# A projection as seven half-size products per pair of units, with its operand sums made by a paired LayerNorm

## The chip, the cores and the metric

The kernel runs on one core of a Trainium2 chip. The metric is device time in microseconds (us) of one execution. The names of the engines are those of the profile: PE is TensorE (matrix products), PEld its weight loads, DVE is VectorE, ACT is ScalarE, POOL is GpSimd and SP is SyncE, which here only issues DMAs. L192 is line 192 of the kernel before.

## The reference, cut to what matters

One inference step of a decoder layer for two request groups with shared weights: a prompt of 1024 tokens and eight samples of eight tokens each, all in fp32. The model width is 1024.

```python
def layernorm(x, g, b):
    mu = mean(x, axis=-1); var = mean(square(x - mu), axis=-1)
    return (x - mu) * rsqrt(var + EPS) * g + b

xn = rmsnorm(x, norm1_g)
q, k, v, glu_a, glu_b, gate_a, gate_b = split(xn @ w_in)
attn = sliding_window_attention(q, k, v)
branch_a = attn @ w_o_attn                            # 1024 x 1024, "o" below
u = glu_a * sigmoid(glu_b)
c = depthwise_conv_31(u)
branch_b = silu(layernorm(c, ln_b_g, ln_b_b)) @ w_pb  # 1024 x 1024, "pb" below
merged = sigmoid(gate_a) * branch_a + sigmoid(gate_b) * branch_b
h = x + merged @ w_out                                # 1024 x 1024, "out" below
y = h + ConvFFN(rmsnorm(h, norm2_g))
```

This is a sketch of the code; a final RMSNorm and the new caches are outputs too.

## The kernel before, in words

All 1024 + 64 tokens are handled together as T = 1088 columns; the 1024 channels lie on 8 tiles of 128 partitions (KT = 8). A matrix product in fp32 is made of three products of fp32r operands: every operand is split into a high part h, made by a cast on ACT, and a low part l, made by a subtraction on DVE (`split_ps`, L224 to L226), and `mm3` (L188 to L192) issues h by h, h by l and l by h. A unit is one tile of 128 output channels with its 128 x 1024 weights. `stream` (L194) runs a unit over the token chunks of 384, 384 and 320 columns (`CHUNKS`), 8 input tiles each, so 72 matmuls; an `evac` function takes each PSUM bank when it is complete. `weight` and `w_split` (L171, L172) load and split the weights of coming units. PSUM has four banks for each of the two tags "mm" and "aux". With the table `QUARTERS` the chunks are four of 272 columns (QW); HALF is 544.

The work is laid out as a list of units for PE. Side work is put on an agenda: `tick` is called once per three matmuls, and `plan` gives steps the tick at which they are emitted. Emission order is the order of priority; `later(n)` gives work a later place by n. Each engine and each DMA queue works strictly in its order.

The stages around the change follow each other on PE:

1. The last gate units of the input projection. Gates and intermediate results go to DRAM (d_ga, d_gb).
2. `phase_y`: eight units "o" (`do_o`, L977). Each multiplies its PSUM chunks with sigmoid(gate_a) and stores the product ma to d_ma on POOL's queue. Beside it runs LayerNorm, as side work in eight blocks of 136 tokens (`ln_steps`): load 8 channel tiles of the conv result from DRAM (d_c, L566), sum over the tiles by three additions (`reduce`, L554), a matmul with a constant matrix for the mean over the 128 partitions (L561), subtraction of the mean (L572), squares on ACT, sums and the second mean matmul, reciprocal root, multiplication (L587), eight Silu activations (L589) and the split into the tiles sh and sl. A block's three steps are 6 and 8 ticks apart, blocks are 15 ticks apart, and the first block begins 4 ticks before the first unit "o".
3. `phase_z`, units "pb" (`do_pb`): each loads its whole row of gate_b (L1011) and of ma (L1014) on SP's queue, 544 KB each, and each chunk's evac multiplies with the sigmoid (L1018), adds ma (L1019) and splits the sum into the quarter tiles mh and ml.
4. Units "out" over quarters: x is loaded per chunk (xr2), added to the PSUM result as H (L1061), and squares are summed for the second RMSNorm. The last four units go chunk by chunk, each chunk followed by `norm2`.
5. The FFN. Its up projection has three plain pairs of units and then 19 Strassen-Winograd pairs: two units are taken as a 2 x 2 matrix of blocks, and seven half-size products on sums of blocks stand for eight. The down projection is done so in part; there the residual H comes back from d_h by accumulating DMAs on POOL's queue (L1434).

## Time and profile before

| | us |
|---|---|
| median of 3 runs | 1664.97 |
| lowest, highest | 1664.64, 1666.62 |
| span of the profiled execution | 1662.4 |
| stage "o" with LayerNorm (637.12 to 735.91) | 98.79 |
| stage pb (735.91 to 830.79) | 94.88 |
| stretch of Strassen-Winograd pairs (1000.00 to 1105.40) | 105.40 |
| PE busy over the span | 1652.5 |

The profile is of one execution, whose own time is the span, from its first to its last instruction; it is 2.6 us shorter than the median, which is a device time of other executions. A stage is bounded by the start of its first matmul and that of the next stage's first. A group row gives the line, engine, operation, output and input, shapes and count, then busy time, mean nanoseconds of one instruction, and the idle time of its engine before them with what ended it. DMA rows give the kilobytes of one transfer and the median time from issue to landing.

### The profile page before, as it was taken

How to read it: one execution, taken by the hardware profiler on the slowest of the kernel's cores; microseconds unless marked ns; L12 is line 12 of the kernel's file. 1: busy time of each engine (PE TensorE's matmuls, PEld its weight loads, DVE VectorE, ACT ScalarE, POOL GpSimd, SP SyncE). 2: the span in 40 equal slices, each digit the busy share in tenths (PEclk: the TensorE clock that was granted, in tenths of full speed). 3: DMA queues.
4: the chain of work that ended last, by engine and by line, in shares of the span. 5: the costliest groups of instructions: out<-in, count | busy, mean ns of one | idle time of the engine just before them, and what ended most of it. 6: DMA issues, size and time to landing. Idle time of an engine off the chain costs nothing.

```text
span 1662.4 us, 29877 instructions
## 1 busy us (share of the span) xinstructions
PE 1652.5 (99%) x11550; PEld 1636.9 (98%) x11550; DVE 1337.3 (80%) x2432; ACT 866.3 (52%) x1781; POOL 290.2 (17%) x483
## 2 busy tenths in 40 slices
PE   9999999999999999999999999999999999999998
PEld 9999999999999999999999999999999999999997
DVE  7899979999989986855545896777887786988867
ACT  6424368774488845973233454444444454524222
POOL 0100112231011111110000171344444320000000
PEclk9999999999999999999999999999999999999999
DMA  6221212232121265544343332244444324766403
GB/s 208 84 71 42 75 60 81 99 103 86 55 53 48 77 227 168 178 154 145 106 155 108 80 125 103 97 113 115 112 114 111 94 103 134 243 168 168 118 14 108
DMA packets 98623, 187.09 MB, mean 113 GB/s; under 512 B 22848, under 2 KB 57680, under 8 KB 98464
## 3 DMA queue, kind: packets, MB, share of 16 engines
q1 hardware_dynamic: 79152, 125.18, 24.3%
q0 software_dynamic: 18896, 59.72, 11.9%
q8 instruction: 91, 1.49, 0.4%
q14 instruction: 52, 0.43, 0.1%
q10 hardware_dynamic: 432, 0.27, 0.1%
HBM read 129.75 MB, written 57.35 MB: 113 GB/s over the span
## 4 chain that ended last, share of the span: by engine, by line
PE 91%; DVE 5%; ACT 2%; DMA 1%; issue 1%; ACTq 0%; DVEq 0%; SPq 0%
PE mm L190 23%; PE mm L192 23%; PE mm L191 23%; PE aux L190 6%; PE aux L192 6%; PE aux L191 6%; PE aux L406 1%; DVE c L520 1%; PE aux L418 1%; PE aux L419 1%; PE aux L396 1%; PE aux L397 1%; DVE bt L520 1%; DVE q L739 1%; DMA bw<-d_b 0%
## 5 line engine op out<-in xcount | busy, mean ns | idle before, releaser
L190 PE MATMUL mm<-xh,whi 128*128 128x384 f32 (+1 forms) x904 | 301.1, 333 | 0.0
L191 PE MATMUL mm<-xl,whi 128*128 128x384 f32 (+1 forms) x904 | 295.4, 327 | 0.1
L192 PE MATMUL mm<-xh,wlo 128*128 128x384 f32 (+1 forms) x904 | 295.4, 327 | 0.0
L191 PEld LDWEIGHTS mm<-xl,whi 128*128 128x128 f32 x904 | 170.0, 188 | 1.6 <-DVE xl L277 0.7
L190 PEld LDWEIGHTS mm<-xh,whi 128*128 128x128 f32 x904 | 169.8, 188 | 0.7
L192 PEld LDWEIGHTS mm<-xh,wlo 128*128 128x128 f32 x904 | 169.7, 188 | 0.1
L190 PE MATMUL mm<-mh,whi 128*128 128x272 f32 (+4 forms) x428 | 125.9, 294 | 0.0
L191 PE MATMUL mm<-ml,whi 128*128 128x272 f32 (+4 forms) x428 | 125.1, 292 | 0.0
L192 PE MATMUL mm<-mh,wlo 128*128 128x272 f32 (+4 forms) x420 | 123.5, 294 | 0.0
L1172 DVE SCALAR_TENSOR_TENSOR acc<-st,fc,acc 128x1104 f32<-128x1104 f32 x88 | 119.8, 1364 | 2.8 <-ACT acc L1170 2.0
L171 ACT CAST whi<-wraw 128x1024 fp32r<-128x1024 f32 (+1 forms) x76 | 74.2, 981 | 79.8 <-PE mm L191 59.7
L520 DVE SCALAR_TENSOR_TENSOR bt<-u,consts,bt 128x513 f32<-128x513 f32 x120 | 89.8, 748 | 0.7
L520 DVE SCALAR_TENSOR_TENSOR c<-sm,hsum,c 128x512 f32<-128x512 f32 x120 | 89.6, 747 | 0.7
L172 DVE TENSOR_TENSOR wlo<-wraw,whi 128x1024 fp32r<-128x1024 f32 (+1 forms) x76 | 86.1, 1136 | 4.9 <-ACT whi L171 4.6
L520 DVE SCALAR_TENSOR_TENSOR c<-u,consts,c 128x512 f32<-128x512 f32 x112 | 83.7, 747 | 0.5
L190 PEld LDWEIGHTS mm<-mh,whi 128*128 128x128 f32 x428 | 80.5, 188 | 0.2
L191 PEld LDWEIGHTS mm<-ml,whi 128*128 128x128 f32 x428 | 80.6, 188 | 0.0
L192 PEld LDWEIGHTS mm<-mh,wlo 128*128 128x128 f32 x420 | 79.0, 188 | 0.0
L1152 POOL COPY st<-co 128x16 f32<-128x16 f32 x44 | 75.6, 1724 | 0.2 <-issue 0.2
L191 PE MATMUL mm<-tl,whi 128*128 128x272 f32 x240 | 69.6, 290 | 0.0
L1320 ACT COPY st<-mm 128x272 f32<-128x272 f32 (+2 forms) x133 | 44.6, 349 | 47.8 <-PE mm L192 47.8
L192 PE MATMUL mm<-th,whi 128*128 128x272 f32 x240 | 69.3, 289 | 0.0
(462 smaller groups left out, 5491.6 us busy)
## 6 DMA issues: line engine op xcount, KB each, us to landing
wraw<-wall SPq DMA_DIRECT2D x118, 512.0 KB, 3.8
bw<-d_b SPq DMA_DIRECT2D x42, 272.0 KB, 3.4
d_b<-gd POOLq DMA_DIRECT2D x36, 272.0 KB, 6.1
d_b<-acc POOLq DMA_DIRECT2D x24, 272.0 KB, 3.3
ar<-wdn SPq DMA_DIRECT2D x32, 192.0 KB, 4.3
d_g<-acc POOLq DMA_DIRECT2D x10, 544.0 KB, 4.3
ga<-d_ga SPq DMA_DIRECT2D x8, 544.0 KB, 4.0
gb<-d_gb SPq DMA_DIRECT2D x8, 544.0 KB, 3.6
```

The source lines that it names most:

```text
L171: self.cast = self.nc.scalar.copy(h[:, z], r[:, z]).ins
L172: self.nc.vector.tensor_tensor(l[:, z], r[:, z], h[:, z].bitcast(F32), ALU.subtract)
L190: mm(ps, wh, xh, start=first, stop=False, skip_group_check=more)
L191: mm(ps, wh, xl, start=False, stop=False, skip_group_check=more)
L192: mm(ps, wl, xh, start=False, stop=last, skip_group_check=more)
L396: nc.tensor.matmul(ps[:, j, :], q[g][:, h, qs], kd[g][:, keys], start=True, stop=False)
L397: nc.tensor.matmul(ps[:, j, :], q[g][:, h, qs], kl[g][:, keys], start=False, stop=True)
L406: nc.tensor.transpose(ps[:, h * P:(h + 1) * P], pt[:, h, kb * P:(kb + 1) * P], self.ident)
L520: mac = lambda o, x, w: nc.vector.scalar_tensor_tensor(o, x, w, o, ALU.mult, ALU.add)
L1152: nc.gpsimd.tensor_copy(ss[:, :, 0:2], co[:, f, 2:].rearrange("p (b t) -> p b t", b=NB))
L1172: nc.vector.scalar_tensor_tensor(acc, st[:, k:k + AW], fw(f, k), acc, ALU.mult, ALU.add)
L1320: op(d, r(ps))
```

## The change

pb becomes Strassen-Winograd's scheme, as in the FFN's up projection. Units 2p and 2p+1 form the output rows, the two halves of the input channels (4 tiles each) the inner blocks and the two halves of the tokens (544 columns) the output columns. Each of four pairs makes seven products; a product is a 128 x 512 block of weights by 512 channels x 544 tokens, done as two quarters of 272 columns, 24 matmuls. The weight operands are A11, A12, A22 and four sums made on DVE (`plan_pair`), each split into one slot of a ring of four, three products ahead. The other operands are the quadrants 11, 21 and 22 of the LayerNorm result and four sums T1 to T4.

LayerNorm makes those: `ln_steps` handles blocks i and i + 4 together, the two token halves at the same place, in 272 columns, and `ln_apply` writes three split quadrants and makes the sums with four subtractions of 544. T1 and T2 stay in SBUF (tiles w0 to w3), T3 and T4 go to DRAM (d_t) on POOL's queue and are loaded back on SP's. All four are split beside pair 0 (`t_split`). The pairs are planned from the start of the last gate unit, 30 ticks apart.

In pb (`pair`) three products are copied to an accumulator row in SBUF by ACT, the others are added on DVE, multiplied with the gate there, and the ma row in DRAM is added by an accumulating DMA on POOL's queue; the split of the result is emitted three products later. The gates come as 32 loads of 272 columns in a ring of five (`gate_load`) with a sigmoid each. In the output projection the first unit takes its quarters in the order 2, 3, 0, 1, x is loaded in whole rows, and H is stored as it is completed.

```diff
+GATE_AFTER = 30
+SPLIT_AFTER = 3
...
-LN_STEPS = (0, 6, 14)
-LN_LEAD = -4
-LN_SPACING = 15
+LN_STEPS = (0, 16, 26)
+LN_SPACING = 30
...
+            ct = live["ct"] = self.t(self.lt, [P, KT, 2 * n], "ct", bufs=2)
+            for x, r in zip(both, each(ct)):
+                nc.sync.dma_start(r, self.d_c[:, :, x * n:x * n + n].rearrange("k p t -> p k t"))
+            for y, r in enumerate(each(ct)):
+                reduce(y, r, self.t(self.cv, [P, 4, n], "u", bufs=2))
...
-            nc.vector.tensor_tensor(ct, ct, ps[:, None, :n].to_broadcast([P, KT, n]), ALU.subtract)
-            sq = self.t(self.cv, [P, KT, n], "c")
-            nc.scalar.activation(sq, ct, AF.Square)
-            reduce(sq, sq)
+            nc.vector.tensor_tensor(ct, ct, ps[:, None, :].to_broadcast([P, KT, 2 * n]), ALU.subtract)
+            for y, r in enumerate(each(ct)):
+                sq = self.t(self.cv, [P, KT, n], "c")
+                nc.scalar.activation(sq, r, AF.Square)
+                reduce(y, sq, sq)
...
+        j, d = i // 2, slice(i % 2 * n, i % 2 * n + n)
+        (r11, r21), (r12, r22) = [[ct[:, 4 * z:4 * z + 4, y * n:y * n + n] for z in range(2)] for y in range(2)]
+        for b, r in (("11", r11), ("21", r21), ("22", r22)):
+            h, l = self.sb[b][j]
+            self.split_ps(h[:, :, d], l[:, :, d], r)
+        w = self.t(self.xw, [P, 2, KT // 2, n], f"w{i}")
+        self.ln_words.append(w)
+        sub = lambda o, x, y: nc.vector.tensor_tensor(o, x, y, ALU.subtract)
+        sub(w[:, 0], r12, r11)
+        sub(r12, r22, r12)
+        sub(w[:, 1], r22, w[:, 0])
+        sub(r21, r21, w[:, 1])
+        nc.gpsimd.dma_start(self.d_t[0, j][:, :, d], r12)
+        nc.gpsimd.dma_start(self.d_t[1, j][:, :, d], r21)
...
+            if n == self.n_in - 1:
+                steps = []
+                for x in range(KT // 2):
+                    steps += self.ln_steps(x, self.now + x * LN_SPACING)
+                self.plan(steps)
...
+              for b in ("11", "22", "21")}
+        self.ln_words = []
+        self.w_stop = self.order.index(("pb", 0))
...
-        steps = []
-        for x in range(KT):
-            steps += self.ln_steps(x, self.now + LN_LEAD + x * LN_SPACING, sh, sl)
-        self.plan(steps)
...
-        def do_pb(m):
-            t = self.t(zt, [P, T], "gb", bufs=2)
-            nc.sync.dma_start(t, self.d_gb[m])
-            nc.scalar.activation(t, t, AF.Sigmoid)
-            r = self.t(zt, [P, T], "mar", bufs=2)
-            nc.sync.dma_start(r, self.d_ma[m])
-
-            def ev(c, o, n, ps):
-                cs = slice(o, o + n)
-                nc.vector.tensor_tensor(t[:, cs], ps[:, :n], t[:, cs], ALU.mult)
-                nc.vector.tensor_tensor(r[:, cs], r[:, cs], t[:, cs], ALU.add)
-                for z, (qo, qn) in enumerate(QUARTERS):
-                    lo, hi = max(o, qo), min(o + n, qo + qn)
-                    if lo < hi:
-                        d = slice(lo - qo, hi - qo)
-                        self.split_ps(mh[z][m // 4][:, m % 4, d], ml[z][m // 4][:, m % 4, d], r[:, lo:hi])
-
-            self.stream(("pb", m), xs, ev)
-
-        for m in range(KT):
-            do_pb(m)
...
+        stage = {}
+        for x in range(2, 4):
+            for j in range(2):
+                stage[x, j] = self.t(mp, [P, KT // 2, QW], f"mh{2 * x + j - 4}1")
+                nc.sync.dma_start(stage[x, j], self.d_t[x - 2, j])
...
+        def t_split(x):
+            for j in range(2):
+                if x >= T3:
+                    tt[x, j] = [self.t(*((xw, [P, KT // 2, QW], f"w{2 * j + y}") if x == T4 else
+                                         (tb, [P, KT // 2, QW], f"t{x}{j}{y}")), F32R) for y in range(2)]
+                h, l = tt[x, j]
+                for z in range(2):
+                    if x < T3:
+                        d, r = (slice(None), slice(None), slice(z * n, z * n + n)), self.ln_words[2 * j + z][:, x]
+                    else:
+                        d = (slice(None), slice(2 * z, 2 * z + 2))
+                        r = stage[x, j][d]
+                    self.split_ps(h[d], l[d], r)
+                    casts.append(self.cast)
+                    lows.append(self.low)
...
+            def split(name, *ops):
+                def go():
+                    if name == "a11":
+                        raws()
+                    for d, x, y, op in ops:
+                        nc.vector.tensor_tensor(live[d], live[x], live[y], op)
+                    i = len(ring)
+                    w = self.t(self.wp, [P, DM], ("whi", "wlo")[i % 2] + str((one + i // 2) % 2), F32R, bufs=1)
+                    with ExitStack() as es:
+                        if i == 2:
+                            es.enter_context(tc.issue_after(casts[3]))
+                            es.enter_context(tc.issue_after(lows[3]))
+                        self.split_ps(w[:, :hw], w[:, hw:], live[name])
+                    ring.append((w[:, :hw], w[:, hw:]))
+                return go
+
+            preps.extend([
+                split("a11"),
+                split("a21", ("a11", "a11", "a21", ALU.subtract), ("a21", "a21", "a22", ALU.add)),
+                split("a21", ("a21", "a22", "a11", ALU.subtract)),
+                split("a21", ("a21", "a12", "a21", ALU.subtract)),
+                split("a11"), split("a12"), split("a22")])
...
+        def gate_load():
+            if len(loaded) < len(gates):
+                m, c = gates[len(loaded)]
+                t = self.t(zt, [P, QW], "gb", bufs=5)
+                nc.sync.dma_start(t, self.d_gb[m][:, c * QW:c * QW + QW])
+                loaded.append(t)
+
+        def gate_open():
+            for _ in range(2):
+                x = len(ready)
+                t = ready[gates[x]] = loaded[x]
+                with tc.issue_after(casts[7]):
+                    nc.scalar.activation(t, t, AF.Sigmoid)
...
+        def pair(p, hooks):
+            acc = [self.t(mp, [P, T], f"ml{2 * (p % 2) + u}1") for u in range(2)]
+            banks = {}
+
+            def place(u, half, j):
+                return acc[u][:, (2 * half + j) * QW:(2 * half + j + 1) * QW]
+
+            def copy(u, half, ps):
+                with tc.issue_after(casts[3]):
+                    for j in range(2):
+                        nc.scalar.copy(place(u, half, j), ps[j])
+
+            def gate(u, half, ps, plain):
+                m, cs = 2 * p + u, slice(half * HALF, half * HALF + HALF)
+                gs = [ready[m, 2 * half + j] for j in range(2)]
+                xs = [place(u, half, j) for j in range(2)]
+                for x, y, g in zip(xs, ps, gs):
+                    if plain:
+                        nc.vector.tensor_tensor(x, y, g, ALU.mult)
+                    else:
+                        nc.vector.tensor_tensor(x, x, y, ALU.add)
+
+                def rest():
+                    if not plain:
+                        for x, g in zip(xs, gs):
+                            nc.vector.tensor_tensor(x, x, g, ALU.mult)
+                    nc.gpsimd.dma_start(acc[u][:, cs], self.d_ma[m][:, cs], accum_op=ALU.add)
+                    gate_load()
+                    gate_load()
+
+                def parts():
+                    for j in range(2):
+                        self.split_ps(*row(m, 2 * half + j), place(u, half, j))
+
+                with self.later(GATE_AFTER):
+                    rest()
+                due.append((7 * p + k + SPLIT_AFTER, parts))
+
+            seq = [
+                ("A", "11", True, 0, 0, copy), ("E", T1, True, 1, 1, copy), ("A", T2, False, 0, 1, copy),
+                ("E", "22", False, 0, 1, gate), ("A", T3, False, 1, 1, gate), ("C", "21", True, 0, 0, gate),
+                ("A", T4, False, 1, 0, gate)]
+            for k, (bank, b, fresh, u, half, op) in enumerate(seq):
+                prep(7 * p + k + 1 + AHEAD)
+                wh, wl = ring[7 * p + k]
+                for j in range(2):
+                    if fresh:
+                        banks[bank, j] = self.bank("mm" if bank == "A" else "aux")
+                    ps = banks[bank, j]
+                    xh, xl = B[b](j)
+                    for x in range(KT // 2):
+                        ks = slice(x * P, (x + 1) * P)
+                        self.mm3(ps[:, :QW], wh[:, ks], wl[:, ks], xh[:, x, :], xl[:, x, :],
+                                 fresh and x == 0, x == KT // 2 - 1, not fresh)
+                op(u, half, [banks[bank, j][:, :QW] for j in range(2)], *((b == T4,) if op is gate else ()))
+                if 2 <= k < 6:
+                    gate_open()
+                for go in hooks.get(k, ()):
+                    go()
+                while due and due[0][0] <= 7 * p + k:
+                    due.pop(0)[1]()
+
...
+        def out_ahead():
+            self.w_hl += [None] * (n_out - len(self.w_hl))
+            self.w_used, self.w_stop, self.slot = n_out, len(self.order), slot
+            self.w_load()
+            self.w_load()
+            self.w_split()
+            for m in range(2):
+                x_load(m)
...
+        for p in range(4):
+            plan_pair(p)
+        for _ in range(5):
+            gate_load()
+        prep(2)
+        t_split(T1)
+        hooks = [{0: [lambda: t_split(T2)], 2: [lambda: t_split(T3)], 4: [lambda: t_split(T4)]}, {},
+                 {2: [lambda: last_rows(2)]}, {2: [lambda: last_rows(3)], 4: [out_ahead]}]
+        for p in range(4):
+            pair(p, hooks[p])
+        while due:
+            due.pop(0)[1]()
...
+        for m in range(KT - OUT_TAIL):
+            for x in (m + 1, *(tail[2 * m - 4:2 * m - 2] if m > 1 else ())):
+                x_load(x)
+            self.stream(("out", m), xm, ev_out(m), chunks=(range(4), (2, 3, 0, 1))[m == 0], table=QUARTERS)
+            nc.gpsimd.dma_start(self.d_h[m], H[m])
```

161 lines of the change are left out of this document (94 added, 67 removed).

## The prediction

> **What bounds the kernel now.** I read the page's busy times first, then the waits of TensorE, then a table of busy times by stage, then the start times of single matmuls at the borders of the changed stage.
>
> ```profile
> span 1662.4 us, 29877 instructions
> ## 1 busy us (share of the span) xinstructions
> PE 1652.5 (99%) x11550; PEld 1636.9 (98%) x11550; DVE 1337.3 (80%) x2432; ACT 866.3 (52%) x1781; POOL 290.2 (17%) x483
> ```
>
> ```profile
> PE mm L629 <- DVE warm L622: 1.1, 1, 1.1
> PE mm L190 <- DVE H L1456: 0.9, 1, 0.9
> PE aux L418 <- ACT pth L225: 0.8, 1, 0.8
> ```
>
> ```profile
> 637.12:735.91 98.79, 98.79 (x610) 98.54 (x609) 75.27 (x108) 88.26 (x127) 12.98 (x24) 1.00 0.47 146
> 735.91:830.79 94.88, 94.88 (x578) 94.88 (x577) 48.28 (x101) 32.36 (x64) 0.54 (x1) 1.00 0.42 140
> ...
> 1000.00:1105.40 105.40, 105.40 (x839) 105.40 (x838) 80.51 (x125) 50.33 (x99) 31.86 (x60) 1.00 0.35 111
> ```
>
> The three wait rows are all the listed waits of TensorE, 2.8 us in the whole span, and none lies near the changed work. So time is matmul issue time, and any wait of TensorE that the change creates is paid in full. The last three rows give, by stage, the length and then the busy time with instructions of PE, PEld, DVE, ACT, POOL: the attention projection with LayerNorm beside it, the projection pb, and a stretch of Strassen-Winograd pairs of the FFN. In all three PE is busy throughout, with the clock at 1.00.
>
> ```profile
> 735.91 0.33 PE L190 MATMUL mm<-sh,whi 128*128 128x384 f32 x1
> 736.09 0.34 PE L191 MATMUL mm<-sl,whi 128*128 128x384 f32 x1
> ...
> 830.64 0.31 PE L192 MATMUL mm<-sh,wlo 128*128 128x320 f32 x1
> 830.79 0.29 PE L190 MATMUL mm<-mh,whi 128*128 128x272 f32 x1
> 830.92 0.29 PE L191 MATMUL mm<-ml,whi 128*128 128x272 f32 x1
> ```
>
> pb runs from 735.91 to 830.79: 576 matmuls (8 units, 3 chunks, 8 input tiles, 3 partial products) in 94.88 us, 0.165 us each. Matmuls overlap: one of 384 columns lasts 0.33 us but the next starts 0.18 us later. Durations must not be multiplied by counts here; stretches must.
>
> **The change, part by part.**
>
> *Matmuls of pb.* Four pairs of seven products of 24 matmuls, 672 of 272 columns, replace 576 of 384 and 320. The FFN row has 839 matmuls, nearly all of 272 columns, in 105.40 us: 0.1256 us each. 672 x 0.1256 = 84.4 us. Saved: 94.88 - 84.4 = 10.5 us. One product takes 3.01 us, a pair 21.1 us. The saving holds as long as TensorE is fed.
>
> *LayerNorm's mean matmuls.* Sixteen of 136 columns become eight of 272: the same columns, taken at nothing; they are TensorE's own work either way, some 0.2 us each now, so at most 1 us either way.
>
> *VectorE and ScalarE in pb.*
>
> ```profile
> L1018 DVE TENSOR_TENSOR gb<-mm,gb 128x384 f32<-128x384 f32 x16 | 8.9, 557 | 23.3 <-PE mm L192 21.2 <-ACT gb L1012 2.1
> L226 DVE TENSOR_TENSOR ml<-mar,mh 128x272 fp32r<-128x272 f32 x15 | 6.6, 439 | 8.3 <-ACT mh L225 8.3
> L225 ACT CAST mh<-mar 128x272 fp32r<-128x272 f32 x15 | 6.1, 410 | 3.8 <-DVE mar L1019 3.8
> L226 DVE TENSOR_TENSOR whi<-s,whi 128x512 fp32r<-128x512 f32 x10 | 6.9, 688 | 12.0 <-ACT whi L225 11.8
> L1264 DVE TENSOR_TENSOR s<-wraw 128x512 f32<-128x512 f32 x6 | 4.1, 691 | 1.9 <-DMA wraw<-wall 1.8
> L1296 DVE TENSOR_TENSOR st<-st,aux 128x272 f32<-128x272 f32 x13 | 5.5, 432 | 1.2 <-PE aux L192 1.2
> L225 ACT CAST whi<-s 128x512 fp32r<-128x512 f32 x10 | 6.2, 624 | 14.7 <-PE mm L192 7.3 <-PE aux L192 4.8 <-issue 2.6
> L1320 ACT COPY st<-mm 128x272 f32<-128x272 f32 x23 | 8.7, 379 | 5.8 <-PE mm L192 5.8
> L554 DVE TENSOR_TENSOR part<-ct 128x544 f32<-128x544 f32 x4 | 2.9, 725 | 7.6 <-DMA ct<-d_c 7.5
> L226 DVE TENSOR_TENSOR sl<-ct,sh 128x1088 fp32r<-128x1088 f32 x3 | 3.9, 1285 | 0.0
> ```
>
> Per pair VectorE gets 4 weight sums (0.691), 7 weight lows (0.688), 14 adds and multiplications of 272 (0.432) and 8 lows of the result (0.439): 2.8 + 4.8 + 6.0 + 3.5 = 17.1 us of 21.1. Around pair 0 come 16 lows of T1 to T4 at about 0.725, 11.6 us. In all 4 x 17.1 + 11.6 = 80 us, some of it before pb starts, against 48.28 us now. ScalarE: 7 casts (0.624), 8 casts and 8 sigmoids of 272 (0.410 each, the sigmoid by the cast), 6 copies (0.379): 13.2 us per pair, plus 16 casts of T at about 0.66. All of it lies beside the matmuls as long as VectorE stays under the stage: 81% per pair here, 76% (80.51 of 105.40) in the FFN pairs, which run without a wait. Without that cover each us of VectorE above 21.1 per pair is paid four times.
>
> *Borders inside pb.* I followed the changed order on each engine with these durations. At the first border the lows of T1 stand on VectorE behind the gate multiplication of the last attention chunk, and the casts of T2 on ScalarE behind the two PSUM copies of product 0, the second of which waits for that product's end (3.0 us into pb). T1 is then ready 0.9 us before its first use; T2's first half 0.5 us before; its second half has a weight split in front of it and comes 0.3 to 0.8 us late. T3 and T4 come from DRAM and are split 1 to 2 us before use. I take a stall of 0.6 us, with 0 and 2 as ends. In pair 1 VectorE has caught up.
>
> *Gate loads and the accumulate.*
>
> ```profile
> gb<-d_gb SPq DMA_DIRECT2D x8, 544.0 KB, 3.6
> mar<-d_ma SPq DMA_DIRECT2D x8, 544.0 KB, 5.4
> xr<-xT SPq DMA_DIRECT2D x32, 136.0 KB, 2.4
> d_b<-gd POOLq DMA_DIRECT2D x36, 272.0 KB, 6.1
> d_b<-acc POOLq DMA_DIRECT2D x24, 272.0 KB, 3.3
> d_g<-acc POOLq DMA_DIRECT2D x10, 544.0 KB, 4.3
> L1434 POOL DMA_DIRECT2D H<-d_h x8: 872/875/901, 1468.4 to 1542.9; - x8
> DMA to landing us min/median/max: 5.4/5.9/9.6
> ```
>
> The gate ring has five buffers for eight quarter rows a pair. The sixth to eighth quarter load only when a buffer is freed, some 6.2 us before use; landing (136 KB, 2.4) and sigmoid (0.4) leave over 3 us. On SP's queue weight loads of the next pair stand behind these gates; they are wanted a pair later. Cost nothing; without the cover, the landing's excess over 5.8 us per pair.
>
> The attention term no longer comes by load (mar) and a VectorE addition but by 16 accumulating DMAs on POOL's queue. The nearest rows are the accumulates into H, 544 KB: 5.4 to 9.6 us, median 5.9 (last two rows). Plain stores lose 1.0 us from 544 to 272 KB (4.3 to 3.3), so I take L = 4.9 for a landing; ends 3.3 and 9.6. The batched d_b<-gd at 6.1 include queueing behind each other. Inside pb the splits that wait for an accumulate are placed three products later, and what stands behind them on VectorE (lows of the next weights) is due two or three products after that: hidden up to L = 9.5. Not hidden is the border to the output projection. Let E be the end of the last product. The next to last half row's DMA is issued at E - 4.0, its splits (1.3 us) stand on VectorE in front of the last gate multiplication, so the last accumulate goes out near E - 2.4 + L and its own splits end near E - 1.2 + 2L. They are wanted at E + 8.7: the first output unit takes chunks 2, 3 first (6.0 us), then 21 matmuls of chunk 0 (2.6). Stall 2L - 9.9, if positive: 0 at 4.9, 1.9 at 5.9, 9.3 at 9.6. As L may as well be 5.4, I take 0.5.
>
> In the page "DMA: Bandwidth & Descriptors" of the Trainium skill, section "Anatomy of one DMA — SWDGE (gpsimd) path", a DMA from GpSimd costs 2.0 us plus bytes over 436 GB/s. By it 272 KB would land in an estimated 2.6 us, the border would be free and the sum 0.5 us lower; the store row of 3.3 us says it is too short here, and no row shows a 272 KB accumulate alone.
>
> *LayerNorm in pairs, one unit earlier.*
>
> ```profile
> 624.16 1.02 SPq L566 DMA_DIRECT2D ct<-d_c  x1
> 627.01 0.73 DVE L554 TENSOR_TENSOR part<-ct 128x544 f32<-128x544 f32 x1 [7.46 <-DMA ct<-d_c]
> 629.59 0.72 DVE L554 TENSOR_TENSOR part<-u 128x544 f32<-128x544 f32 x1
> 642.64 0.47 PE L561 MATMUL aux<-red,mean 128*128 128x136 f32 x2
> L589 ACT ACT_TABLE_LOAD x8 | 10.3, 1283 | 0.1
> ```
>
> Per pair of blocks VectorE gains four subtractions of 544 (2.9 us) and loses about 0.5 on splits (three of 544 against two of 1088): +2.4, about 10 us over all, while half the table loads of ScalarE go. The attention stage stands at 75.27 of 98.79 on VectorE, and part of the first pairs moves ahead of 637: room for it. The first mean matmul now sits 27 matmuls (4.0 us) before 637.12, at 633.1; the sum it reads is ready after the third load (issued 624.16, landing by 630.7 if as slow as the slowest of these took, then additions) near 631.9: spare 1.2 us. The second mean comes near 641.4 with its operand ready between 641.3 and 641.6: 0.2 us. The eight stores of T3, T4 on POOL stand between the 24 ma stores and feed loads that start only at pb. Later means have 1 us or more.
>
> *Output projection and after.* Whole-row x loads and more, smaller d_h stores change no order on TensorE beyond the chunk order; the x rows are loaded a unit ahead. Nothing, against at most one DMA landing of 4 us if a row were late.
>
> *Sum.* -10.5 + 0.6 + 0.5 + 0.2 = -9.2; with 0.2 for the mean matmuls' unknown, -9.0. The profiled execution's span is 1662.4, so 1653.4 there; it stands 2.6 us under the median of 1664.97, which becomes 1656.0.
>
> **The rivals.**
>
> *Accumulates land late (slower).* The splits on VectorE wait for them in order. Beyond L = 9.5 the third and fourth accumulate of a pair delay the lows of the next pair's weights: a stall of about 2L - 19 in three pairs, beside 2L - 9.9 at the end. With the other stalls (1.0) the saving is gone when 8L = 76.4, L = 9.6, the largest value of the H row; slower past 0.2% from L = 10. At twice the median, 11.8, it is 13.7 + 13.8 + 1.0 - 10.5 = +18.0, 1683. For it: the 9.6 of the H row was reached beside the same sort of matmul stage. Against: the median, and half the bytes. In the page "SBUF — State Buffer" of the Trainium skill, section "SBUF: two separate sides", a DMA from GpSimd is starved while VectorE runs a two-port copy, 620 ns turning into 3100; by that estimate L grows by 2.5 to 7.4, and the time by 4.4 over the forecast (1660.4). The page infers that tensor-tensor operations, VectorE's work here, don't do it, and the issue row of 872 to 901 ns beside such additions agrees.
>
> *VectorE or the borders eat more (still faster).* VectorE waits for ScalarE's casts at each split: the L226 row of pb shows 8.3 us idle over 15. If that costs 0.5 us at each of 15 splits, a pair comes to 24.6, above 21.1, but ring and order absorb most of it; with the late first mean (a landing of 7 instead of 6.5, plus a second) I price it at 3 to 6 us over the forecast: 1659 to 1661.6.
>
> *The change saves little.* If a 272-column matmul fed by halves of two tiles cost 0.139 instead of 0.1256, nothing would be left at 93.4 + 1: 1664. Against it, the FFN row is of the same operands and width.
>
> **How the numbers follow.** Forecast (stalls 0 to 3 us): 0.62, range 1654.5 to 1658.5. Borders and VectorE: 0.20. Little saved: 0.05. Accumulates or another wait in front of TensorE, slower: 0.13. The bound of telling from no change is 0.2%, 3.3 us: faster 0.82, same 0.05, slower 0.13. The range begins at 1653.5 (no stalls, 1654.5, less a us for the matmul rate) and goes up to 1665, which takes in the first three cases.
>
> **What would show it.** Right: a stage of 84.4 to 87 us between the first matmul on the quadrant tiles and the first on the merged ones, with VectorE near 80% of each pair; waits of TensorE on a low of T2 under 1 us; L near 5 in the DMA list; attention stage unchanged. Wrong: a wait of several us of the first output unit on a split behind an accumulate; waits on weight lows in every pair; a mean matmul waiting on a load.

## The result: slower, and where the time went

The changed kernel takes 1674.80 us in the median (1673.08 to 1675.51, 4 runs), the kernel before 1664.81 (1664.06 to 1666.62, 4 runs). The ratio is 1.0056, interval 1.0041 to 1.007. The prediction, 1656.0 and faster, is wrong in sign, and the time lies outside its range of 1653.5 to 1665: 9.0 us were to be gained and 10.0 were lost.

### The profile after

From here on L numbers are those of the changed kernel's own lines (the helpers moved by one). First the page's busy times of the changed kernel:

```profile
span 1673.3 us, 30193 instructions
PE 1648.1 (98%) x11630; PEld 1628.9 (97%) x11630; DVE 1366.8 (82%) x2482; ACT 867.6 (52%) x1806; POOL 315.5 (19%) x523
```

PE is busy 4.4 us less than before and the span is 10.9 us longer: the matmuls were saved, and waits took their place. The waits of TensorE say on what (total us, times, longest):

```profile
PE mm L191 <- ACT t L226: 4.2, 2, 3.8
PE aux L566 <- DVE sm L559: 3.5, 4, 1.6
PE aux L191 <- ACT ml L1133: 2.4, 3, 2.0
PE mm L192 <- DVE t L227: 2.1, 1, 2.1
PE mm L191 <- DVE H L1642: 1.7, 2, 0.9
```

The first row is the border to the output projection, the second LayerNorm's mean matmuls, the third and fourth lie in pb, the last in the FFN's down projection. Busy times of the changed kernel by stage, in the columns used in the prediction: the attention stage, pb, the first 96 matmuls of the output projection.

```profile
637.55:740.27 102.72, 99.25 (x592) 97.42 (x591) 80.04 (x112) 67.96 (x90) 18.87 (x32) 1.00 0.48 157
740.27:833.25 92.98, 86.88 (x675) 85.08 (x673) 66.49 (x134) 49.94 (x118) 12.64 (x15) 1.00 0.68 173
833.25:852.30 19.05, 14.81 (x99) 13.97 (x97) 7.89 (x17) 6.79 (x15) 1.72 (x2) 0.82 0.83 244
```

And the same 96 matmuls in the kernel before:

```profile
830.79:842.90 12.11, 12.11 (x99) 12.11 (x98) 5.01 (x9) 2.69 (x6) 0.00 (x0) 1.00 0.53 168
```

| us | before | after | difference | predicted |
|---|---|---|---|---|
| up to the first matmul of "o" | 637.12 | 637.55 | +0.4 | 0 |
| attention stage | 98.79 | 102.72 | +3.9 | +0.4 |
| pb | 94.88 | 92.98 | -1.9 | -9.9 |
| first 96 matmuls of "out" | 12.11 | 19.05 | +6.9 | +0.5 |
| the rest (span less the above) | 819.5 | 821.0 | +1.5 | 0 |

These add to +10.9, up to rounding. The small fall in pb hides the whole forecast saving: 24 matmuls with nothing in their way take 3.02 to 3.03 us, 28 such products 84.7, against a forecast of 84.4. The other 8.3 us of pb are stalls: 2.4 at product 3 of pair 0 (T2), the rest in pairs 1 to 3.

*The attention stage.* VectorE's timeline in the changed kernel ahead of the longest of the four waits on a sum, then the mean matmul (start, duration, engine, line, instruction, idle time before and its releaser):

```profile
692.27 0.73 DVE L559 TENSOR_TENSOR u<-ct 128x544 f32<-128x544 f32 x1 [1.71 <-DMA ct<-d_c]
692.91 1.85 DVE L353 RECIPROCAL bt<-bt 128x272 f32<-128x272 f32 x1
694.97 2.41 DVE L595 TENSOR_TENSOR ct<-ct,bt 128x2176 f32<-128x2176 f32 x1
698.15 1.22 DVE L173 TENSOR_TENSOR wlo<-wraw,whi 128x1024 fp32r<-128x1024 f32 x1
700.10 0.29 DVE L559 TENSOR_TENSOR sm<-u 128x136 f32<-128x136 f32 x1
```

```profile
700.53 0.70 PE L566 MATMUL aux<-sm,mean 128*128 128x272 f32 x2 [1.59 <-DVE sm L559]
```

Ahead of the sum stand a wait for the load of the conv rows, the reciprocal and the multiplication of the pair before, and a low part of weights. Which of them makes it late is tried below.

*T2.* Timeline of VectorE in the changed kernel (start, duration, engine, line, instruction, idle time before and its releaser):

```profile
746.08 0.69 DVE L227 TENSOR_TENSOR wlo<-wraw,wlo 128x512 fp32r<-128x512 f32 x1
749.18 1.36 DVE L227 TENSOR_TENSOR t<-w,t 128x544 fp32r<-128x544 f32 x2 [2.41 <-DMA d_ma<-ma]
```

The low of T2 waits neither for ScalarE nor for LayerNorm but for a store of ma. Its tile was given the space of the last ma chunk, which was still on its way to DRAM.

*Pairs 1 to 3.* Groups of ScalarE between 760 and 834 us in the changed kernel, then its timeline and TensorE's at the longest of these stalls:

```profile
L1119 ACT ACTIVATE gb<-gb 128x272 f32<-128x272 f32 x26 | 11.1, 431 | 12.4 <-DMA gb<-d_gb 10.6 <-DVE ml L1143 1.2 <-DVE mh L227 0.3
L226 ACT CAST mh<-ml 128x272 fp32r<-128x272 f32 x24 | 9.0, 417 | 11.5 <-DMA ml<-d_ma 11.5
L1133 ACT COPY ml<-mm 128x272 f32<-128x272 f32 x12 | 4.4, 383 | 0.0
```

```profile
819.97 0.74 ACT L226 CAST mh<-ml 128x272 fp32r<-128x272 f32 x2 [2.18 <-DMA ml<-d_ma]
820.62 0.67 ACT L1133 COPY ml<-aux 128x272 f32<-128x272 f32 x2
```

```profile
818.80 0.29 PE L193 MATMUL mm<-t,wlo 128*128 128x272 f32 x1
821.05 0.39 PE L191 MATMUL aux<-220h,whi 128*128 128x272 f32 x1 [1.96 <-ACT ml L1133]
```

ScalarE stands still 11.5 us in front of casts that wait for an accumulate and 10.6 in front of sigmoids that wait for a gate load. The copies of PSUM never wait themselves (0.0), since they stand behind these. The next product adds into the copied bank, so TensorE waits for a 0.4 us copy that waits for a transfer it has nothing to do with.

*The border.* Accumulates on POOL, and TensorE, in the changed kernel; the last product ends at 833.25:

```profile
829.90 0.86 POOL L1149 DMA_DIRECT2D ml<-d_ma  x1 [16.24 <-ACT gb L1119]
832.08 0.86 POOL L1149 DMA_DIRECT2D ml<-d_ma  x1 [1.32 <-DVE ml L1143]
837.83 0.86 POOL L1149 DMA_DIRECT2D ml<-d_ma  x1 [4.89 <-DVE ml L1148]
842.24 0.86 POOL L1149 DMA_DIRECT2D ml<-d_ma  x1 [3.55 <-DVE ml L1141]
```

```profile
836.77 0.29 PE L193 MATMUL mm<-t,110l 128*128 128x272 f32 x1
840.82 0.59 PE L191 MATMUL mm<-t,110h 128*128 128x272 f32 x1 [3.76 <-ACT t L226]
841.30 0.59 PE L192 MATMUL mm<-t,110h 128*128 128x272 f32 x1
841.69 0.43 PE L193 MATMUL mm<-t,110l 128*128 128x272 f32 x1
```

The second of the four is issued at 832.08, and ScalarE's cast waits for it until 840.35: 8.2 us, with the DMA engines 97% busy from 830 to 836. TensorE stands still from 836.77 to 840.82. After that a matmul of 272 columns starts every 0.23 us instead of 0.125, at a granted clock of 0.50. The first accumulate was late for another reason, on VectorE:

```profile
827.12 1.23 DVE L173 TENSOR_TENSOR 110l<-wraw,110h 128x1024 fp32r<-128x1024 f32 x1 [2.67 <-ACT 110h L172]
828.26 0.43 DVE L1143 TENSOR_TENSOR ml<-ml,aux 128x272 f32<-128x272 f32 x1
```

The low of the first output unit's weights waits for ScalarE, which waits 3.13 us for the weights' load. The gate work behind it is held up.

### The profile page after: what moved, and what is told of

Same layout as the page of the kernel before. It is cut to its first block, busy times and chain, and to the rows that moved or that the text cites. A ratio compares the mean times of both kernels' runs of the same rounds, so it can differ in the third digit from the quotient of the medians.

```text
span 1673.3 us, 30193 instructions
## 1 busy us (share of the span) xinstructions
PE 1648.1 (98%) x11630; PEld 1628.9 (97%) x11630; DVE 1366.8 (82%) x2482; ACT 867.6 (52%) x1806; POOL 315.5 (19%) x523
## 4 chain that ended last, share of the span: by engine, by line
PE 47%; issue 3%; DMA 2%; DVE 2%; ACT 1%; POOL 0%; DVEq 0%; POOLq 0%; ACTq 0%
PE mm L192 10%; PE mm L191 10%; PE mm L193 10%; PE aux L193 6%; PE aux L191 6%; PE aux L192 5%; DMA ml<-d_ma 1%; DMA bw<-d_b 1%; DMA wraw<-wall 0%; POOL ml L1149 0%; DVE ml L227 0%; DVE w L1262 0%; DVE H L1699 0%; PE aux L1256 0%; ACT mh L226 0%
## 5 line engine op out<-in xcount | busy, mean ns | idle before, releaser
L191 PE MATMUL mm<-mh,whi 128*128 128x272 f32 (+4 forms) x348 | 102.3, 294 | 0.0
L193 PE MATMUL mm<-mh,wlo 128*128 128x272 f32 (+4 forms) x340 | 100.0, 294 | 0.0
L192 PE MATMUL mm<-ml,whi 128*128 128x272 f32 (+4 forms) x332 | 98.1, 296 | 0.0
L172 ACT CAST whi<-wraw 128x1024 fp32r<-128x1024 f32 (+1 forms) x66 | 63.7, 971 | 64.9 <-PE mm L192 54.3
L173 DVE TENSOR_TENSOR wlo<-wraw,whi 128x1024 fp32r<-128x1024 f32 (+1 forms) x66 | 73.7, 1120 | 4.1 <-ACT whi L172 3.7
L193 PE MATMUL mm<-th,whi 128*128 128x272 f32 x240 | 69.3, 289 | 0.0
L191 PE MATMUL mm<-th,whi 128*128 128x272 f32 x240 | 69.1, 288 | 0.0
L374 ACT ACTIVATE p<-p,nm 128x257 f32<-128x257 f32 (+1 forms) x128 | 62.3, 490 | 11.9 <-DVE nm L369 11.5
L191 PEld LDWEIGHTS mm<-mh,whi 128*128 128x128 f32 x348 | 65.5, 188 | 0.0
```

What stands on the lines that cost most here:

```text
L172: self.cast = self.nc.scalar.copy(h[:, z], r[:, z]).ins
L173: self.nc.vector.tensor_tensor(l[:, z], r[:, z], h[:, z].bitcast(F32), ALU.subtract)
L191: mm(ps, wh, xh, start=first, stop=False, skip_group_check=more)
L192: mm(ps, wh, xl, start=False, stop=False, skip_group_check=more)
L193: mm(ps, wl, xh, start=False, stop=last, skip_group_check=more)
L374: nc.scalar.activation(pt[:, j, lo:width + 1], pt[:, j, lo:width + 1], AF.Exp, bias=nm[:, j:j + 1], scale=-1.0, accum_out=den[:, j:j + 1])
```

## The experiments

Two theories to begin with. Q: an instruction that waits for a late transfer or partner holds up what stands behind it on its in-order engine; each stall is one such hand-off, and goes when the order changes, with the same work on the same engines. C: VectorE and the DMA engines have too much to do; another order only moves the stalls. Where I compare, it is by stage in the profiled execution of each kernel. One caution: eight kernels with the attention stage as changed (the changed one and those that alter only later parts) start pb between 740.3 and 742.4 us, mean 741.7. So its growth is nearer to 5 us than to the 3.9 above, and differences of 2 us there tell nothing. pb scatters more: in the nine kernels that leave its own instructions as changed (with another LayerNorm or another output projection) it takes 90.5 to 96.0 us, and T2's product 3.4 to 6.3. Of the experiments only the combined kernels and e_pool were run several times. Beside the first four single runs (e_ln, e_t2, e_outlate, e_tail) the kernel before took 1668.76, 4 us over its median, so the totals of single runs tell little.

### pb: the order on ScalarE, the accumulates, T2's place

**e_act**: sigmoids and casts of finished half rows are queued behind the PSUM copies, and the casts come two products later.

```diff
-SPLIT_AFTER = 3
+SPLIT_AFTER = 5
...
-                with tc.issue_after(casts[7]):
+                with tc.issue_after(self.copied):
                     nc.scalar.activation(t, t, AF.Sigmoid)
...
-                        nc.scalar.copy(place(u, half, j), ps[j])
+                        self.copied = nc.scalar.copy(place(u, half, j), ps[j]).ins
...
-                        self.split_ps(*row(m, 2 * half + j), place(u, half, j))
+                        with tc.issue_after(self.copied):
+                            self.split_ps(*row(m, 2 * half + j), place(u, half, j))
```

> Only the order on ScalarE inside pb is changed: the sigmoids of the gates and the casts of the finished half rows, which wait for a load or an accumulating DMA, are queued behind the PSUM copies of the product that is emitted with them, and the casts come two products later. Theory Q: pairs 1 to 3 stall because PSUM copies stand on ScalarE behind operations that wait for a transfer; those stalls (5.5 to 9 us in the runs so far) fall under 1.5 us, pb without pair 0 comes to 63.5 to 65 us, total 4 to 7 us under the changed kernel. Theory C: the same work on the same engines, so waits on lows of weights take the place, and less than 1.5 us is gained.

```profile
742.24:828.39 86.15, 85.00 (x674) 84.78 (x673) 65.25 (x136) 51.20 (x122) 12.70 (x15) 1.00 0.77 191
```

pb takes 86.15 us instead of 92.98. All 28 products take 3.02 to 3.03 us but T2's (4.44). Busy times of VectorE and ScalarE are as before within 1.3 us, so Q holds here and C does not: 86.15 lies far below the 90.5 to 96.0 of the kernels with the old order, and in the combined kernels, which have this order too, no product of pairs 1 to 3 waits either. In e_act the casts no longer wait for an accumulate (0.0 us), while the sigmoids still wait 10.0 us for gate loads. Which of the two moves of the casts did it, behind the copies or two products later, was not tried apart. The time was 1668.55, the span 1666.6, 6.7 us less.

**e_noacc**: the accumulating DMA is left out.

```diff
-                    nc.gpsimd.dma_start(acc[u][:, cs], self.d_ma[m][:, cs], accum_op=ALU.add)
```

> The accumulating DMAs are left out, so the attention term is missing from the sum that the output projection reads; nothing else is changed. It prices everything that hangs on these transfers. If accumulates are the main cause in pb and at the border: the stalls of pairs 1 to 3 fall by more than half, the border falls from 6.9 to under 1.5 us, total 8 to 11 us under the changed kernel. If the gate loads hold up ScalarE instead: the stalls of pairs 1 to 3 fall by less than a third. Theory C: pb stays over 90 us.

```profile
741.91:827.26 85.35, 85.01 (x674) 84.79 (x673) 67.78 (x140) 53.95 (x126) 0.54 (x1) 1.00 0.51 155
827.26:839.36 12.10, 12.10 (x99) 12.10 (x98) 5.79 (x11) 3.80 (x9) 0.00 (x0) 1.00 0.70 244
```

1661.06 us, and a span 14.0 us under the changed kernel's, more than the 8 to 11 expected. Without accumulates the stalls of pairs 1 to 3 and the whole border are gone. ScalarE's groups of e_noacc between 760 and 827 us:

```profile
L1119 ACT ACTIVATE gb<-gb 128x272 f32<-128x272 f32 x27 | 11.4, 430 | 10.8 <-DMA gb<-d_gb 10.8
L226 ACT CAST mh<-ml 128x272 fp32r<-128x272 f32 x22 | 8.7, 416 | 6.5 <-DVE ml L1148 6.4
```

The sigmoids stand ahead of the copies as in the changed kernel and wait as long for gate loads (10.8 us against 10.6), and TensorE does not stall. So the gate waits alone cost nothing. Together with e_act: the accumulates set off the stalls in pb, and the place of the casts that wait for them decides whether they are paid.

**e_t2**: the tiles of T2 are made last, so that T3 and not T2 gets the space of the ma chunk.

```diff
...
-        for x in range(2):
+        for x in (T1, T3, T2):
```

> Only the places in SBUF are exchanged: the split of T2 no longer lies where the last ma chunk waits for its store, the split of T3 does. Q: the 2.2 us stall inside the third product of pair 0 falls under 0.5 us, the rest of pb is unchanged, total 1.5 to 2.2 us under the changed kernel. C: VectorE, which has to split T1 to T4 there, is late at T3 or at the third pair instead; total gains under 0.7 us.

T2's stall is gone (3.03 for the product, 5.38 in the changed kernel), but pb stays at 92.89: the products of the later pairs take up to 6.11 now. The total was 1676.29, so the gain that Q expected is missing, as C had it. Whether the later stalls grew because this one went is not shown: pb's own scatter is larger than T2's stall. In the combined kernels, which have this edit, T2's product takes 3.03 as well.

### The border

**e_outlate**: the weight low of the first output unit is queued behind the gate multiplication.

```diff
-                            nc.vector.tensor_tensor(x, x, g, ALU.mult)
+                            self.mult = nc.vector.tensor_tensor(x, x, g, ALU.mult).ins
...
-            self.w_split()
+            with tc.issue_after(self.mult):
+                self.w_split()
```

> Only one order is changed: the low part of the first output unit's weights (it waits for a load that comes late) is queued on VectorE behind the gate multiplication of the product before the last but one, not ahead of it. Q, with VectorE's queue as the cause at the border to the output projection: the first two accumulates of the last pair go out about 3 us earlier, the stalls of the first output unit (5.6 us with the slow clock after it 6.9) fall to 2 to 3.5 us. If transfers that share the DMA engines are the cause instead: accumulates still land after 5 to 8 us and the border stays within 1.5 us of 6.9. C: border unchanged.

1672.61 us; the 96 matmuls take 14.54 instead of 19.05, 2.4 more than before, as Q expected with VectorE's queue as the cause. The first accumulate now leaves 7.5 us ahead of pb's end (828.31 against 835.79) instead of 3.4.

**e_tail**: the x rows of the last four output units are loaded behind the later weights.

```diff
-            self.nc.sync.dma_start(r, self.a["wall"][i])
+            self.w_dma = self.nc.sync.dma_start(r, self.a["wall"][i]).ins
...
-            for x in (m + 1, *(tail[2 * m - 4:2 * m - 2] if m > 1 else ())):
-                x_load(x)
+            if m + 1 not in tail:
+                x_load(m + 1)
...
+        with tc.issue_after(self.w_dma):
+            for m in tail:
+                x_load(m)
```

> Only the four x rows of the last output units, 544 KB each, are loaded later, behind weights of the output projection, instead of at the end of pb, where two of them run beside the last accumulates. If shared DMA time is the cause at the border: the second accumulate of the last pair lands in about 5 us instead of 8, and the border falls from 6.9 to 3 to 4.5 us. If VectorE's queue is the cause: the accumulates go out as late as before and less than 1.5 us is gained. C: unchanged.

16.56 us for the border, 4.5 more than before, and the second accumulate lands 5.7 us after its issue (834.12 to 839.85) instead of 8.2, both about as expected if shared DMA time is a cause. So the DMA load of that time is a part of it, beside VectorE's queue; 1675.02 in all.

**e_border**: quarters 2 and 3 of the first two output units come before quarters 0 and 1 of both.

```diff
...
+                for cs in ((2, 3), (0, 1)):
+                    for x in range(2):
+                        self.stream(None, xm, ev_out(x), chunks=cs, w=two[x], table=QUARTERS)
...
```

> Only the order of the first two output units is changed: token quarters 2 and 3 of both units come before quarters 0 and 1 of both, so the half rows finished last are wanted 12 us after pb instead of 6. If the accumulates' landing is the border's cause: the part of the border that waits for the first half rows of the last pair goes; the part that waits for quarters 2 and 3 stays, since they are wanted as early as before. The border falls from 6.9 us to 3 to 5 us. If TensorE waits there for something else: unchanged.

A miss: 19.20, unchanged, with waits of 0.63 and 3.52 for the rows of quarters 2 and 3. The first two accumulates decide, not the last ones.

### The attention stage: plan, order, stores, work

**e_ln, e_ln2, e_ln3**: other plans of LayerNorm's steps (the third gives each pair its own ticks).

```diff
-LN_STEPS = (0, 16, 26)
-LN_SPACING = 30
+LN_STEPS = (0, 18, 28)      # e_ln, spacing 33; e_ln2: (0, 16, 28), spacing 35
+LN_STEPS = ((0, 16, 33), (34, 52, 76), (77, 100, 124), (125, 150, 172))      # e_ln3
```

> Only the plan of the paired LayerNorm is stretched: its second and third steps come 18 and 28 ticks after the first instead of 16 and 26, and pairs are 33 ticks apart instead of 30. Theory Q (hand-offs: single waits in the engines' in-order queues, each behind a transfer or an operation placed too early, stop TensorE, and each stall goes when its own cause goes): the four waits of mean matmuls on sums, 3.5 us in the changed kernel, fall under 1 us, the first pb matmul comes near 737.5 instead of 740.3, and the total is 2 to 3.5 us shorter than the changed kernel's 1673.3 us span. Theory C (capacity: VectorE and ScalarE are too full in these stages, so that a removed wait comes back at the next place): the waits move to later mean matmuls or to the first products of pb, and less than 1 us is gained.

> The plan of LayerNorm again, with another part of it stretched. In the kernel with steps 18 and 28 and a spacing of 33 ticks nothing was gained, and there the loads of the third and fourth pair of blocks waited on SP's queue for the stores of T3 and T4 of the pair two before, whose buffer they take over. Here the steps are 16 and 28 and the spacing is 35, so that from the second step of one pair to the first mean of the pair two after it there are 58 ticks instead of 50 (28 to 86 against 26 to 76). Theory Q: the waits of mean matmuls on sums fall from 3.5 us or more to 1.5 or less, and the total by 2 to 3 us against the changed kernel (span 1673.3). Theory C: they stay above 3 us.

> Each step of the paired LayerNorm gets its own tick, so that on TensorE the second to last mean matmuls stand 18 to 37 matmuls (3 to 6 us) later than in the changed kernel. In the earlier two plans the ticks had been stretched too, but the mean matmuls had moved by only 0 to 17 matmuls and the sums had moved with them. Theory Q: a mean matmul stops TensorE because it stands in the queue ahead of the point at which its sum is really there; given 3 us more, the waits on sums fall from 3.5 to 5.3 us to under 1.5 us, and the first pb matmul comes at 736.5 to 738. Theory C: VectorE is behind in the whole stage, and the waits stay at 3 us or more, or the first products of pb wait instead.

Misses all three: waits of the mean matmuls 3.4, 4.8 and 4.2 us, pb starts at 740.53, 741.95 and 742.40, times 1675.95, 1676.61 and 1680.58. With e_ln3 T1 is late as well (first products 5.04 and 5.41).

**e_lnord**: the subtractions and the stores of T3 and T4 go ahead of two of the three splits.

```diff
-        for b, r in (("11", r11), ("21", r21), ("22", r22)):
+        def split(b, r):
...
+        split("21", r21)
...
         nc.gpsimd.dma_start(self.d_t[1, j][:, :, d], r21)
+        split("11", r11)
+        split("22", r22)
```

> Only the order inside a LayerNorm pair is changed: the split of quadrant 21 first, then the four subtractions and the stores of T3 and T4, then the splits of 11 and 22. The stores free the buffer for the loads of the pair two later, so those loads start some 1.5 us earlier. If the loads behind the stores make the sums of the third and fourth pair late: their first mean matmuls (waits of 0.7 and 1.6 us in the changed kernel, up to 1.8 in others) wait under 0.5 us. If VectorE is behind instead: no change.

A miss: waits 5.0 us, pb at 743.46, 1680.69. The loads of the next pairs were issued at 661.15 and 687.88 against 661.91 and 686.90, the first 0.8 us earlier, the second 1.0 later. So the edit did not do what it was made for, and says little about the stores.

Three runs then took one suspect each away: F the stores that hold the load buffer, W VectorE's work, and C, here another C, the round trip through ScalarE.

**e_nostore, e_nosub, e_onesq**:

```diff
...
-        nc.gpsimd.dma_start(self.d_t[0, j][:, :, d], r12)      # e_nostore and e_nosub
-        nc.gpsimd.dma_start(self.d_t[1, j][:, :, d], r21)
-        sub(r12, r22, r12)                                     # e_nosub
-        sub(r21, r21, w[:, 1])
...
-                nc.scalar.activation(sq, r, AF.Square)
+                if y == 0:                                     # e_onesq
+                    nc.scalar.activation(sq, r, AF.Square)
-                reduce(y, sq, sq)
+                reduce(y, (sq, r)[y], sq)
```

> Left out: the stores of T3 and T4 to DRAM; what is loaded in their place is a part of the conv result. All LayerNorm arithmetic stays. Theory F (the buffer of the conv rows comes free only when the last store of a pair has landed, so the loads of the third and fourth pair are late): loads at some 656 and 682 instead of 661.9 and 686.9, the first mean matmuls of pairs 2 and 3 (0.73 and 1.59 us in the changed kernel) wait for nothing, waits on the sums 1.2 us or less instead of 3.5, pb starts at 737.9 or earlier. Theory W (VectorE's work of a pair is too long for the order in which it is queued) and theory C (the round trips between VectorE, ScalarE and TensorE in a pair): waits 3 us or more, pb starts at 740 or later.

> Left out: as in the run before, and the two subtractions that make T3 and T4 (0.73 us each, 1.45 us of VectorE a pair). Theory W: waits on the sums fall by about 1.5 us a pair against the run before, to 1.5 us or less, and only here. Theory F: as the run before, within 0.5 us. Theory C: 3 us or more in both.

> Left out: the squares of the second block of each pair (the variance of that block is not formed; the additions run on the centred values instead), so that one ScalarE pass and the wait for the single buffer of squares are gone; the stores stay. Theory C: the second mean matmuls (0.68 and 0.48 us in the changed kernel) wait for nothing, and with the shorter chain the later first means too: waits 1.5 us or less, pb starts at 738.5 or earlier. Theories F and W: the first means of pairs 2 and 3 still wait, 2.3 us together or more, pb starts at 739.5 or later.

Windows of the attention stage in e_nostore, and in e_nosub:

```profile
637.58:740.87 103.29, 99.39 (x592) 97.29 (x591) 80.31 (x112) 68.16 (x90) 13.01 (x24) 1.00 0.42 135
```

```profile
637.74:737.69 99.95, 98.55 (x592) 97.31 (x591) 75.44 (x104) 67.02 (x89) 13.02 (x24) 1.00 0.42 139
```

Without stores the loads go out 3 us earlier (658.62, 684.20) and nothing is gained: waits 3.9, so F falls. Without the two subtractions VectorE does 4.9 us less and the stage is 3.3 us shorter; the waits fall to 1.4, and pb starts at 737.69, 2.6 us below the lowest of the eight. With one square pass less pb starts at 739.12, 1.1 us below the lowest of the eight, with waits of 2.6. There the first mean matmul of the fourth pair no longer waits, and its second waits 0.99, which neither W nor C expected: the round trip through ScalarE has a share, smaller than that of the subtractions and not much larger than the scatter. So in the main it is VectorE's work that stands in front of the sums, W, at only 78% mean use of VectorE in this stage. Each of the three is one execution, and e_nosub's stage is still 1.2 us longer than before. The spans were 1671.3, 1669.5 and 1670.2.

### Together

**e_comb**: e_act, e_t2, e_outlate, e_tail and the plan of e_ln2. **e_comb2**: these with e_ln3's plan and e_border. **e_comb3**: e_act, e_t2, e_outlate and e_border, the plan and the x rows as in the changed kernel.

> All single edits together: the plan of LayerNorm with spacing 35, T2's place away from the ma chunk, the order on ScalarE, the late low part of the first output weights and the later x rows. Theory Q: the stalls go with their causes, some 14 of the 19 us that separate the result from the forecast: attention stage at 737.5, pb 85.5 to 87, border 1 to 3, total 1656 to 1662 us, ratio 0.995 to 0.998 of the kernel before. Theory C: 1670 us or more.

> The edits together that gained or are expected to: LayerNorm steps with ticks of their own, T2's place, the order on ScalarE, the late low part of the first output weights, the later x rows, and quarters 2 and 3 of two output units ahead of 0 and 1. Theory Q: pb 84.8 us as with the earlier set, attention stage within 2 us of the kernel before, border under 1.5 us: total 1655 to 1659 us, ratio 0.993 to 0.997 of the kernel before. Theory C: 1664 us or more.

> The edits that worked, and no others: T2's place away from the ma chunk, the order on ScalarE, the late low part of the first output weights, and quarters 2 and 3 of two output units ahead of 0 and 1. LayerNorm's plan and the x rows stay as in the changed kernel. Theory Q: pb 84.8 us, border under 1.5 us, no stall at 870 us (in the set before, the moved x rows came late there), attention stage 4 to 6 us longer than before as in every run: total 1659 to 1662 us, ratio 0.996 to 0.9985 of the kernel before. Theory C: the border or pb takes the gain back, 1665 us or more.

e_comb, between the two theories: 1668.48, ratio to the kernel before 1.0016 (1.0006 to 1.0026). pb is down to 84.75 with no stall, but the border takes 18.10: one gap of 3.07 us and half the clock after it. e_comb2, a miss for Q: 1670.01, 1.0024 (1.0014 to 1.0034). The border is free (12.77), but the later x rows cost a gap of 3.27 us, with a slow clock after it, so that the other 672 matmuls of the output projection take 93.20 us instead of 87.00; T1 is late by e_ln3's plan. The windows of e_comb3:

```profile
637.53:741.14 103.61, 99.30 (x592) 97.46 (x591) 80.15 (x112) 68.28 (x90) 18.83 (x32) 1.00 0.48 156
741.14:825.90 84.76, 84.76 (x675) 84.76 (x674) 65.58 (x137) 51.07 (x122) 12.71 (x15) 1.00 0.77 191
825.90:838.11 12.21, 12.21 (x99) 12.14 (x97) 5.24 (x10) 2.97 (x6) 1.72 (x2) 1.00 0.97 287
```

1662.8 us (1661.61 to 1665.29, 11 runs), the kernel before 1665.89 beside it: ratio 0.9982, 0.9973 to 0.9991. The ratio is in the expected range, the time 0.8 us above it. This version is faster than both kernels, by 3.1 us of the 9.0 forecast. Against the kernel before pb is 10.1 us shorter, the border 0.1 longer, the attention stage 4.8 longer, and the rest 3.5 longer, of which 0.9 lies in the other 672 matmuls of the output projection (87.92 against 87.00) and 1.2 in waits for H in the FFN's down projection (2.1 against 0.9); the other 1.4 are open. The profiled execution's span of 1661.1 is thus 1.3 us under that of before, less than the medians differ.

**e_pool**: e_comb3, with the subtractions for T3 and T4 on GpSimd.

```diff
-        sub(r12, r22, r12)
+        nc.gpsimd.tensor_tensor(r12, r22, r12, ALU.subtract)
...
-        sub(r21, r21, w[:, 1])
+        nc.gpsimd.tensor_tensor(r21, r21, w[:, 1], ALU.subtract)
```

> The order changes of e_comb3 (T2's place, the late weight low, the order on ScalarE, the order of the output units), and the two subtractions that make T3 and T4 on GpSimd's engine instead of VectorE; nothing is left out. Theory W (VectorE's work in the order given holds up the sums of the attention stage): VectorE has 5.8 us less there, waits on the sums 2 us or less instead of 4.3, pb starts at 738 to 739 instead of 741.1, and the median falls from 1662.8 by 2 to 3 us to 1660 to 1661 (before at some 1665.7), provided that a subtraction on GpSimd takes under 3 us; if it takes more, the stores and the next load come later and half of that is lost. If W is wrong, pb starts at 740.5 or later and the median stays at 1662 to 1664.

A miss: 1669.19, ratio 1.0019 (1.001 to 1.0028); pb starts at 749.08, and the mean matmuls wait 9.4 us. One GpSimd subtraction takes 1.7 us. VectorE's groups between 637.61 and 749.08 of e_pool show what it does beside it, and those of the changed kernel's attention stage the same splits without it:

```profile
L227 DVE TENSOR_TENSOR 110l<-ct,110h 128x544 fp32r<-128x544 f32 x2 | 3.8, 1880 | 0.0
L559 DVE TENSOR_TENSOR c<-c 128x272 f32<-128x272 f32 x8 | 5.3, 656 | 0.2
```

```profile
L227 DVE TENSOR_TENSOR 110l<-ct,110h 128x544 fp32r<-128x544 f32 x2 | 1.4, 718 | 0.0
L559 DVE TENSOR_TENSOR c<-c 128x272 f32<-128x272 f32 x8 | 3.5, 438 | 0.1
```

VectorE's instructions beside a GpSimd subtraction are stretched to as much as 2.6 times, so the 5.8 us taken off it (eight subtractions of 0.73) come back: 82.49 us busy in that stage, 80.15 in e_comb3. And the ma stores stand behind the subtractions on POOL:

```profile
715.66 0.56 DVE L1004 TENSOR_TENSOR ma<-mm,ga 128x384 f32<-128x384 f32 x1 [3.32 <-DMA d_ma<-ma]
```

VectorE waits for such a store to free the ma buffer, and the next mean matmul waits 4.66 us: a hand-off of kind Q again. That VectorE has less to do was not achieved here, so this run says nothing against W.

## Why the prediction was wrong, step by step

- *Matmuls of pb, -10.5.* Right: 3.02 to 3.03 us per product against 3.01, and 84.76 us for the stage once nothing waits (e_comb3) against 84.4. "The change saves little" falls.
- *VectorE and ScalarE in pb.* The loads were right in size: VectorE 66.5 of 93 us. But cover was reckoned by busy time. In e_act the same engines with the same work feed TensorE without a stall. "VectorE or the borders eat more" had part of the mechanism (stalls at hand-offs) but put it on VectorE and at 3 to 6 us; the stalls in the pairs came by ScalarE.
- *"Hidden up to L = 9.5".* This is the step that failed in pb. L itself was right: a median of 4.8 us against the 4.9 taken, shortest 4.1, longest 8.2. But the working followed only VectorE's queue. On ScalarE the casts that wait for an accumulate, and the sigmoids that wait for a gate, stand in front of the PSUM copies that release a bank for the next product. That cost about 6 us in three pairs. The casts that wait for an accumulate are what counts: without accumulates the sigmoids waited as long (10.8 us) and TensorE did not stall. So the gate ring at "nothing" came out as far as e_noacc shows, but by luck: landings were 3.1 us in the median but up to 7.6, where 2.4 was taken.
- *T2, 0.6 with 0 to 2 as ends.* 2.4 (0.3 to 3.3 in the nine kernels of the caution above), for a reason the working did not hold: a tile's space, and the store that still read it.
- *Border, 0.5.* 6.9. The formula looked at the last two accumulates and took the next to last to leave at E - 4.0; it left at E + 4.6 (837.83, E = 833.25). What decided was the second of the four: out at E - 1.2, landed 8.2 us later, wanted at E + 3.5 by the last input tile of the first output unit's first chunk, which takes a quarter that the working had as ready. Even at L = 4.9 and with a cast of 0.4 it would have been some 0.6 us late. Some 2 us more are the slow clock after the gap: the 16 matmuls from 840.82 to 844.85 take 4.03 us, at 0.125 each they would take 2.0.
- *LayerNorm, 0.2, "later means have 1 us or more".* Four waits, 3.5 us: 0.7 at the second mean, where 0.2 was taken, and 2.8 at three later ones. The stage grew by about 5 us by the mean of eight kernels. The extra VectorE work was counted (2.4 us a pair) and set against its idle time over the stage, not against what stands in front of the next sum. e_nosub shows this to be the main cause, with a smaller share of ScalarE's squares (e_onesq); another plan and the stores left out gained nothing.
- *The rest, nothing.* +1.5, not resolved; the wait for H in the FFN's down projection (1.7 against 0.9) is a part.
- *"Accumulates land late"*, the slower rival, had the right places (the pairs and the border) and the right transfers, but saw VectorE's splits held up where it was ScalarE's copies. Its point of decision was wrong too: at a median of 4.8 the kernel was already slower.

Not tried: a third buffer for the conv rows and a longer gate ring.

## What to carry to other kernels

Before costing an instruction at nothing because its engine has idle time, write down, for each in-order engine, what stands behind every instruction that waits for a transfer, and who waits for that: a 0.4 us copy behind a cast that waits for a DMA cost more here than any sum of busy times suggested. A queue's wait is no cost in itself: 10.8 us of waiting for gates cost nothing where no cast waited for an accumulate. Look too at which transfer still reads the space that a new tile is given. Judge such a change by the stage that it touches and against the scatter of that stage in kernels that leave it alone: here a stall of 2.4 us could be taken away without the stage getting shorter.
